# An early small write to the output: 128 rows in place of 16

**Chip, cores, metric.** One core of one Trainium2 chip. The metric is the device time of one execution in microseconds (us); lower is better.

## The reference

```python
def reference(x, y):                      # both (32, 256, 1024) float32
    batch, seq, dim = x.shape
    result = np.zeros((batch, seq, dim * 2), dtype=np.float32)
    result[..., 0::2] = x
    result[..., 1::2] = y
    return result
```

It interleaves two arrays. There is nothing to compute: 67.1 MB are read, 67.1 MB are written.

## The kernel before

The flat arrays are cut into 8 blocks of 128 rows of 8,192 elements. A block's x and y are loaded by SyncE's queue (SP), VectorE (DVE) copies them into every second place of an output tile, half a block at a time, and ScalarE's queue (ACT) stores that tile. x, y and output tiles have two buffers each. Ahead of the loop stands the small write that this study is about: zeros on top of the first store's rows, which the first store overwrites later.

```python
    wpool = ctx.enter_context(tc.tile_pool(name="wp", bufs=1))
    zero = wpool.tile([16, 128], fp32, name="zero")
    nc.vector.memset(zero, 0.0)
    first = dataclasses.replace(of, offset=0, ap=[[2 * WL, 16], [1, 128]])
    nc.scalar.dma_start(out=first, in_=zero)                  # L47

    start = 0
    for lw in lwidths:                                        # 8 blocks
        # ... tiles of this block, xs and ys: its rows in x and y
        nc.sync.dma_start(out=xtile, in_=xs)                  # L56
        nc.sync.dma_start(out=ytile, in_=ys)                  # L57
        soff = 0
        while soff < lw:                                      # 2 halves
            # ... otile, and os_: its 128 rows of 32,768 B in the output
            nc.vector.tensor_copy(out=otile[:, 0::2], in_=xsub)   # L70
            nc.vector.tensor_copy(out=otile[:, 1::2], in_=ysub)   # L71
            nc.scalar.dma_start(out=os_, in_=otile)               # L72
            soff += width
        start += P * lw
```

The program sets the semaphores by itself: the first store waits for the early write's landing, as both write the same rows.

## Time and profile before

| What | Before |
|---|---|
| time, 3 runs | 315.98 us median (315.83 to 316.15) |
| span of the profiled run | 313.8 us |
| VectorE busy | 72.8 us, 23% |
| DMA moved | 134.23 MB, 428 GB/s over the span |
| first store issued, its first packet | 24.32 us, 29.10 us |

The span is that of one profiled execution; the time has some 2 us more around it. VectorE, the only engine that computes, is idle for three quarters of the span, so the DMA engines, which move the data, are left to set this time. The prediction shows the lines behind it.

### The profile page before, as it was taken

What the parts mean: (1) busy time and instruction counts of PE and PEld (TensorE: products, weight loads), DVE (VectorE), ACT (ScalarE), POOL (GpSimd) and SP (SyncE); (2) the same over time, 40 slices, a digit from 0 to 9 for tenths busy, and PEclk for the clock granted to TensorE, in tenths of its full rate; (3) what the DMA queues carried; (4) which work ended last, traced back from release to release, by engine and by line L of the source; (5) the groups of instructions that cost most, each with busy time, mean ns of one, the idle gap of its engine ahead of it and who ended that gap; (6) DMA issues with size and microseconds to landing.
All of it is one profiled execution on the core that took longest, in us unless ns stands there. A gap on an engine that the chain in (4) does not pass through costs nothing.

```text
span 313.8 us, 152 instructions
## 1 busy us (share of the span) xinstructions
DVE 72.8 (23%) x33; POOL 0.2 (0%) x4
## 2 busy tenths in 40 slices
DVE  0433002231032410325003150130501305023500
POOL 0000000000000000000000000000000000000000
DMA  8999999999999999999999999999999999999997
GB/s 339 464 405 397 468 401 464 405 464 405 464 405 464 405 459 409 451 418 451 418 434 434 430 439 426 443 413 455 401 468 401 468 401 468 401 468 401 464 405 334
DMA packets 4640, 134.23 MB, mean 428 GB/s; under 512 B 528, under 2 KB 544, under 8 KB 544
## 3 DMA queue, kind: packets, MB, share of 16 engines
q1 hardware_dynamic: 2304, 67.11, 49.9%
q10 hardware_dynamic: 2336, 67.12, 49.5%
HBM read 67.11 MB, written 67.12 MB: 428 GB/s over the span
## 4 chain that ended last, share of the span: by engine, by line
DMA 83%; DVE 11%; DVEq 1%; issue 0%
DMA out_dram<-otile 76%; DMA ytile<-in_y_dram 7%; DVE otile L71 6%; DVE otile L70 5%; DVEq L83 1%; DVEq L70 0%
## 5 line engine op out<-in xcount | busy, mean ns | idle before, releaser
L70 DVE COPY otile<-xtile 128x4096 f32<-128x4096 f32 x16 | 36.6, 2295 | 184.9 <-DMA out_dram<-otile 173.7
L71 DVE COPY otile<-ytile 128x4096 f32<-128x4096 f32 x16 | 36.6, 2292 | 39.8 <-DMA ytile<-in_y_dram 39.8
L45 DVE MEMSET zero<- 16x128 f32 x1 | 0.2, 165 | 0.9 <-PEq L119 0.9
L119 POOL MEMSET const-bfloat16-1.0<- 128x1 bf16 x1 | 0.1, 102 | 0.0
L119 POOL MEMSET const-uint8-127<- 128x1 uint8 x1 | 0.1, 102 | 0.0
L119 POOL MEMSET const-float32-0.0<- 128x1 f32 x1 | 0.1, 99 | 0.2 <-issue 0.2
L119 POOL MEMSET const-float32-1.0<- 128x1 f32 x1 | 0.1, 99 | 0.0
## 6 DMA issues: line engine op xcount, KB each, us to landing
out_dram<-otile ACTq DMA_DIRECT2D x16, 4096.0 KB, 29.1
xtile<-in_x_dram SPq DMA_DIRECT2D x8, 4096.0 KB, 43.6
ytile<-in_y_dram SPq DMA_DIRECT2D x8, 4096.0 KB, 60.7
out_dram<-zero ACTq DMA_DIRECT2D x1, 8.0 KB, 6.3
```

Source lines behind the costliest of these rows:

```text
L45: nc.vector.memset(zero, 0.0)
L70: nc.vector.tensor_copy(out=otile[:, 0::2], in_=xsub)
L71: nc.vector.tensor_copy(out=otile[:, 1::2], in_=ysub)
L83: tc.compile()
L119: nc = _bacc.Bacc("TRN2", target_bir_lowering=False, num_devices=1)
```

## The change

The early write is to cover every row that the first store writes. The intent is presumably to warm something on the way to the output: with 16 rows the early write touched only 16 of the 128 rows that the first store writes, one packet for each of the 16 DMA engines; with 128 rows it touches them all, eight packets for each.

```diff
-    zero = wpool.tile([16, 128], fp32, name="zero")
+    zero = wpool.tile([P, 128], fp32, name="zero")
     nc.vector.memset(zero, 0.0)
-    first = dataclasses.replace(of, offset=0, ap=[[2 * WL, 16], [1, 128]])
+    first = dataclasses.replace(of, offset=0, ap=[[2 * WL, P], [1, 128]])
     nc.scalar.dma_start(out=first, in_=zero)
```

## The prediction

> **What bounds the kernel now.** I first read the page of the profile from the top, to see which engine is full.
>
> ```profile
> span 313.8 us, 152 instructions
> DVE 72.8 (23%) x33; POOL 0.2 (0%) x4
> ...
> DMA  8999999999999999999999999999999999999997
> ...
> DMA packets 4640, 134.23 MB, mean 428 GB/s; under 512 B 528, under 2 KB 544, under 8 KB 544
> ...
> q1 hardware_dynamic: 2304, 67.11, 49.9%
> q10 hardware_dynamic: 2336, 67.12, 49.5%
> ```
>
> VectorE, the only engine that computes, works 23% of the span. The 16 DMA engines are at 90% or more in 38 of the 40 slices, and the two queues (q1 has the loads, q10 the stores) together fill 99.4% of their time. So the kernel is bound by the bytes that it moves, and a wait somewhere else matters only if it leaves the DMA engines with nothing queued.
>
> The packet records of the trace say how tight that is. There are 4,096 packets of 32,768 B (one row of a tile each, 256 on each engine), and nearly all of them took 1.213 us: 32,768 B / 1.213 us = 27.0 GB/s on one engine, 432 GB/s on sixteen. 256 x 1.213 = 310.5 us is therefore the floor for this traffic at this rate. What the span has above that floor is 3.3 us. I looked for it by stretches of the span; the last two columns are the DMA share and the rate (a packet counts where it starts, so short stretches are uneven and the share can pass 1).
>
> ```profile
> 0.90:2.50 1.60, 0.13 (x1) 0.00 (x0) 1.00 1.20 328
> ...
> 11.30:25.80 14.50, 8.30 (x4) 0.00 (x0) 1.00 1.01 434
> 25.80:28.00 2.20, 0.69 (x1) 0.00 (x0) 1.00 1.39 477
> 28.00:30.00 2.00, 0.00 (x0) 0.00 (x0) 1.00 0.61 262
> ...
> 60.00:300.00 240.00, 59.02 (x26) 0.00 (x0) 1.00 1.00 433
> 300.00:313.80 13.80, 0.00 (x0) 0.00 (x0) 1.00 0.88 380
> ```
>
> From 60 to 300 us it runs at 433 GB/s with a share of 1.00: nothing to win. Two places are slow. One is the start: the first packet starts 0.99 us in, and the first round of load packets takes 1.47 to 2.27 us instead of 1.213. The other is the moment of the first big store: packets that start between 25.8 and 27.7 us take up to 1.88 us. By the packet records the time above 1.213 us is 0.71 us per engine in the first place (21 packets) and 0.64 us in the second (21 packets), and nowhere else is a big packet off 1.213 by more than 5 ns. The start (0.99), these two (1.35), the end (the last packet ends at 312.7 of 313.8, so 1.1) and the small packets account for the 3.3 us to within rounding.
>
> So the whole stretch that an early write to the output could possibly mend is the 0.64 us around the first store. Next, how the early write lies in the opening; the columns are start, length, engine, line and operation.
>
> ```profile
> 0.86 0.17 DVE L45 MEMSET zero<- 16x128 f32 x1 [0.86 <-PEq L119]
> 1.06 0.42 ACTq L47 DMA_DIRECT2D out_dram<-zero  x1
> ...
> 12.28 4.50 DVE L70 COPY otile<-xtile 128x4096 f32<-128x4096 f32 x2 [11.25 <-DMA xtile<-in_x_dram]
> 16.80 0.33 SPq L56 DMA_DIRECT2D xtile<-in_x_dram  x1
> 22.00 4.50 DVE L71 COPY otile<-ytile 128x4096 f32<-128x4096 f32 x2 [5.22 <-DMA ytile<-in_y_dram]
> 24.32 2.56 ACTq L72 DMA_DIRECT2D out_dram<-otile  x2
> ```
>
> ```profile
> out_dram<-zero ACTq DMA_DIRECT2D x1, 8.0 KB, 6.3
> ```
>
> The early write is issued at 1.06 us and lands 6.3 us later, near 7.4 us. ACT's queue holds the first store back until that landing (its semaphore wait ends at 7.42 us), because both write the same rows. But the first store cannot be issued before its second copy, which starts at 22.00 us when y has landed, is done at 24.3 us. The wait has 24.3 - 7.4 = 16.9 us of slack.
>
> **What the Trainium skill says.** All four places are on the page "DMA: Bandwidth & Descriptors".
> - "Where 436 GB/s comes from" gives 435.2 GB/s as the ceiling of 16 ports. The trace agrees: 432 GB/s in the packet records.
> - "Queues, rings and completion order": each engine goes round-robin between queue rows, a packet at a time. The trace agrees. Before 5.27 us an engine has only load packets; there each engine takes one 512 B packet of q10 in 27 ns, then one load packet of 1.213 us, then the 4 B semaphore packet at 6.50 us. During the first store, q10 and q1 alternate one 32 KB packet each.
> - "Why a DMA increments its semaphore by 16 and not by 1": the number of engines is the largest up to 16 that divides the slowest dimension on both sides. 16 rows give 16 engines with one row each, 128 rows give 16 engines with eight. The trace of before has 16 early packets and 16 increments; the 128-row case is seen in the big stores.
> - "Specifications" calls 512 B the smallest transfer at line rate, below which there is a read-modify-write. The new rows are still 512 B, so no new penalty should appear; before's took 27 ns each.
>
> **The change part by part.**
> 1. The memset goes from 16 to 128 partitions with 128 elements in each. Length per partition is the same, so I expect about 0.17 us again. Even ten times that would be nothing on the path, as VectorE idles until 12.28 us.
> 2. The DMA instruction on ACT: 0.42 us for 16 rows; the 128-row stores take 0.34 to 0.36 us. No gain or loss; ACT idles until 24.3.
> 3. The packets: 112 more of 512 B, 7 more on each engine, at 27 ns: 7 x 0.027 = 0.19 us of DMA time on every engine. It is the one term that lies on the path, because the engines are full before and after. It goes wholly to the time: +0.19 us.
> 4. The landing. If each row takes a turn between two load packets (0.027 + 1.213 = 1.24 us a turn), the seven further rows put the landing 7 x 1.24 = 8.7 us later: 15.0 us after issue, near 16.1 us. That is 8 us ahead of 24.3, so the first store's issue isn't delayed. Effect: 0.
> 5. The warming. The old write touched rows 0 to 15, one per engine, so not the rows that each engine then stores; the new one touches all 128 rows of the first store. If the 0.64 us of stretched packets come from a first touch of those rows, up to -0.64 us. I doubt it. All 16 engines are stretched alike, whether or not their rows were near the 16 already written; later stores also go to rows that nothing has touched, and their packets all take 1.213 us; and the early write itself cost the loads beside it nothing (1.211 to 1.226 us). I give it one chance in five, worth on average -0.1 us.
>
> Sum: 315.98 + 0.19 - 0.1 = 316.07, rounded to 316.1 us.
>
> **The rivals.**
> - *The cold write path is warmed row by row*: the first store's packets keep to 1.213 us, and the time is 315.98 + 0.19 - 0.64 = 315.5 us. For it: the stretch stands exactly where the first big store begins, as the other one stands at the first load. Against it: point 5.
> - *The cost is only moved*: the new rows do the first touch at 5 to 16 us, the load packets there stretch by the same 0.64 us, and the time stays at 316.2. For it: DMA is full then too, so a stall cannot hide.
> - *The early write becomes the wait that holds the first store.* If each small row must let two load packets pass, as the first one did, eight turns of 2.45 us end at about 5.3 + 19.6 = 24.9 us, and the store is issued 0.5 to 1 us late. Even so the DMA engines have the second pair of loads queued until 34 us, so nothing idles and the order merely shifts: 316.2 to 316.5. To cost 2% (6.3 us) the landing would have to slip past 34 us by as much again. Alternation one by one in the store phase speaks against even the mild form.
> - *The eight rows of an engine go as one packet*: landing stays near 6.3 us after issue, the same +0.19 us or somewhat less. The time can't tell this from my main line; the landing can.
>
> **Range and chances.** The known terms run from -0.45 (warming in full) to +0.5 (a delayed store). The three runs of before spread over 0.32 us by themselves, so 315.5 to 316.6 us should hold the result eight times in ten. A 2% gain would need 6.3 us, almost twice everything the span has above its floor of 310.5 us, so I give it 0.5%; a 2% loss needs DMA engines that idle for 6 us or small rows that cost thirty times their 27 ns: 1%.
>
> **What would show each step right or wrong.** In the changed kernel's profile: 4,752 packets (112 more) and 656 under 2 KB; q10 with 2,448; the early write at 64.0 KB with about 15.0 us to landing (6 to 8 would mean bursts, over 23 that it holds the store); the first issue of a store at 24.3 to 24.6 us; the stretched packets just before the first store's still summing to about 0.6 us per engine (gone if warming works, found at 5 to 16 us if moved); and a span of about 314.0. The prediction is wrong if the stretch is gone and the time is under 315.6, if the loads between 5 and 16 us slow by more than the 0.19 us, or if the rate of 433 GB/s in the middle of the span changes, for which I see no cause.

## The result

| | Before | After |
|---|---|---|
| time, 6 runs each | 316.12 us (315.83 to 316.93) | 316.24 us (315.71 to 317.0) |
| ratio after to before, 95% interval | | 0.9999 (0.9981 to 1.0017) |
| span of the profiled run | 313.8 us | 314.4 us |

A ratio here is the mean time of one kernel's fast runs over that of the other's of the same rounds, so it isn't quite the ratio of the medians above. The time is the same. The page of the changed kernel, in the lines that answer to those of before:

```profile
span 314.4 us, 152 instructions
...
DMA packets 4752, 134.29 MB, mean 427 GB/s; under 512 B 528, under 2 KB 656, under 8 KB 656
...
q1 hardware_dynamic: 2304, 67.11, 49.9%
q10 hardware_dynamic: 2448, 67.18, 49.5%
...
L45 DVE MEMSET zero<- 128x128 f32 x1 | 0.2, 165 | 0.9 <-PEq L119 0.9
...
out_dram<-zero ACTq DMA_DIRECT2D x1, 64.0 KB, 14.0
```

There are 112 packets more (4,752 against 4,640), all on q10 and all under 2 KB. The memset takes the same 165 ns for eight times the rows. The early write lands 14.0 us after its issue, not 6.3. Its packets took 27 ns each as before: the small packets' records sum to 0.51 us per engine, against 0.32, which is the 0.19 us of the prediction.

The opening by order of time (start, length, engine, line, operation):

```profile
1.07 0.40 ACTq L47 DMA_DIRECT2D out_dram<-zero  x1
...
12.61 4.50 DVE L70 COPY otile<-xtile 128x4096 f32<-128x4096 f32 x2 [11.57 <-DMA xtile<-in_x_dram]
...
22.31 4.50 DVE L71 COPY otile<-ytile 128x4096 f32<-128x4096 f32 x2 [5.20 <-DMA ytile<-in_y_dram]
24.64 2.56 ACTq L72 DMA_DIRECT2D out_dram<-otile  x2
```

The early write is down at 15.1 us and the first store is issued at 24.64 us, so it still waits for its own copy and not for the early write. It comes 0.3 us later than before because y does.

**How the stretch is read.** The last two load packets on each engine ahead of the first store took longer than 1.213 us. The stretch is this time above 1.213 us, summed over the packets and divided by the 16 engines. To see it in the page's form, take a window in which exactly these 32 packets start; the last figure of a queue's line is the time of its packets as a share of 16 engines' window. Before, from 25.8 to 28.0 us:

```profile
q1 hardware_dynamic: 32, 1.05, 139.2%
```

After, from 25.8 to 28.3 us:

```profile
q1 hardware_dynamic: 32, 1.05, 130.0%
```

Before: 1.392 x 2.2 us x 16 / 32 = 1.531 us a packet, two per engine, so 2 x (1.531 - 1.213) = 0.64 us of stretch. After: 1.300 x 2.5 x 16 / 32 = 1.625 us, so 0.82 us. The stretch has not gone; in this profile it is 0.2 us longer. It is the one figure that the change was to make smaller.

### The profile page after: what moved, and what is told of

It is laid out like the page before. It is cut to its first block, busy times and chain, and to the rows that moved or that the text cites. A ratio compares the mean times of both kernels' runs of the same rounds, so it can differ in the third digit from the quotient of the medians.

```text
span 314.4 us, 152 instructions
## 1 busy us (share of the span) xinstructions
DVE 72.8 (23%) x33; POOL 0.2 (0%) x4
## 2 busy tenths in 40 slices
DMA packets 4752, 134.29 MB, mean 427 GB/s; under 512 B 528, under 2 KB 656, under 8 KB 656
## 4 chain that ended last, share of the span: by engine, by line
DMA 83%; DVE 11%; DVEq 1%; issue 0%
DMA out_dram<-otile 76%; DMA ytile<-in_y_dram 7%; DVE otile L71 6%; DVE otile L70 5%; DVEq L83 1%; DVEq L70 0%
## 6 DMA issues: line engine op xcount, KB each, us to landing
out_dram<-otile ACTq DMA_DIRECT2D x16, 4096.0 KB, 29.1
xtile<-in_x_dram SPq DMA_DIRECT2D x8, 4096.0 KB, 43.6
```

## The experiments

Eleven further runs were made, nine of them of new kernels. The stretch is given by the packet records, per engine.

**1. The same kernels again.** No edit. The repeat of before is a single run, so its state is unknown (314.1 us of span and a time of 315.89 us put it beside the fast ones).

> The kernel before, unchanged, for the spread of the profile itself. In the first two profiles the load packets ahead of the first store were stretched by 0.64 us per engine (before) and 0.82 us (after). Theory A (the stretch is what a starting stream costs, and has nothing to do with the early write): here again 0.5 to 0.9 us, not necessarily 0.64. Theory B (the number of early rows changes it): 0.64 within 0.05. Time 315.7 to 316.9.

Measured: stretch 0.59 us. That lies within what both theories allow, so it only shows the spread.

> The changed kernel against the one before, with more rounds, for the size of the time difference and a second profile. Main theory: plus 0.19 us (112 more packets of 27 ns over 16 engines), ratio 1.0006, which five rounds may not part from 1; stretch 0.5 to 0.9 us and its difference to before not repeated. Rival (the stretch is really longer after the change): 0.82 us again, and the time up by 0.3 to 0.4 us (ratio 1.001).

Measured: ratio 0.9997 (0.9985 to 1.0009), stretch 0.96 us, span 314.4 us. A rise by more than 0.1%, as the rival had it, is outside the interval; the 0.06% of the main theory is inside, and so is nothing at all. The longer stretch did repeat, which the main theory did not expect.

**2. No early write at all.**

```diff
-    zero = wpool.tile([P, 128], fp32, name="zero")
-    nc.vector.memset(zero, 0.0)
-    first = dataclasses.replace(of, offset=0, ap=[[2 * WL, P], [1, 128]])
-    nc.scalar.dma_start(out=first, in_=zero)
```

> No early write at all. Theory A: the early write warms nothing, so the stretch before the first store is 0.5 to 0.9 us as with it, the start packets are as before, and the time is that of before less one packet of 27 ns: ratio 0.999 to 1.001. Theory B (the first touch of the output is dear and the 16 rows already took most of it away): the stretch or the delay from the first store's issue to its first packet (4.8 us in before) grows by 1 us or more and the time with it, ratio 1.003 or more.

Measured: ratio 1.0 (0.9987 to 1.0012), span 313.7 us, first store issued at 24.32 us and its first packet at 29.00 us, 4.7 us later as in before. The window from 25.8 to 28.0 us:

```profile
q1 hardware_dynamic: 32, 1.05, 137.1%
```

1.371 x 2.2 x 16 / 32 = 1.508 us a packet, 0.59 us of stretch. Theory B falls: the 16 rows of before did nothing either. The small write is idle weight in both kernels, and the simplest of the three has none.

**3. The 128 rows elsewhere.** The early write goes to the rows of the fifteenth of the sixteen stores.

```diff
-    first = dataclasses.replace(of, offset=0, ap=[[2 * WL, P], [1, 128]])
+    first = dataclasses.replace(of, offset=2 * (total - P * WL), ap=[[2 * WL, P], [1, 128]])
```

> The 128 early rows go into the place of the second last store's rows, so the first store finds none of its rows touched and is not held by their landing; the number of packets is that of the changed kernel. Theory A: stretch 0.5 to 0.9 us, time as the changed kernel's, ratio to before 1.000 to 1.001. Theory B (rows warm their own addresses): stretch before the first store as in the run without an early write and above that of before, and something shorter at the second last store, whose packets are all 1.213 us already.

Measured: ratio 0.9995 (0.9981 to 1.001), stretch 0.87 us, nothing at the fifteenth store. Whether the rows touched are the first store's own makes no difference: 0.82 and 0.96 us with them, 0.87 without.

**4. Eight small packets per engine, on 16 rows.** To tell the number of packets from the number of rows as the reason for the longer stretch.

```diff
+    SEGS = 8
-    zero = wpool.tile([P, 128], fp32, name="zero")
+    zero = wpool.tile([16, SEGS * 128], fp32, name="zero")
     nc.vector.memset(zero, 0.0)
-    first = dataclasses.replace(of, offset=0, ap=[[2 * WL, P], [1, 128]])
-    nc.scalar.dma_start(out=first, in_=zero)
+    first = dataclasses.replace(of, offset=0, ap=[[2 * WL, 16], [256, SEGS], [1, 128]])
+    nc.scalar.dma_start(out=first, in_=zero.rearrange("p (s e) -> p s e", s=SEGS))
```

> Eight early pieces of 512 B on each of 16 rows: as many small packets per engine as in the changed kernel (8), on as few rows as in before. The stretch before the first store was 0.59 to 0.64 us per engine with 0 or 1 early packets per engine, and 0.82 to 0.96 with 8. Theory (the number of small packets shifts the engines against each other): stretch 0.8 to 1.0 us, profiled span 314.2 to 314.5. Rival (the number of rows, so of addresses, does it): 0.55 to 0.65 us, span 313.7 to 314.2. Time within 0.15% of before in either case.

Measured: stretch 0.60 us, span 313.9 us, ratio 0.9991 (0.9974 to 1.0008). The window from 25.8 to 28.0 us:

```profile
q1 hardware_dynamic: 32, 1.05, 137.6%
```

The theory falls; the rival's figures hold. With no early write or 16 small rows the stretch was 0.59, 0.59, 0.60 and 0.64 us, with 128 small rows 0.82, 0.87 and 0.96. Why more rows should lengthen it isn't settled, and one run below (16 big rows, 0.80 us) fits neither group. The ratios can't tell the 0.25 us apart, as their intervals are wider.

**5. Four pieces on each of the 128 rows.** The landing is pushed past the point at which the first store is ready.

```diff
+    SEGS = 4
-    zero = wpool.tile([P, 128], fp32, name="zero")
+    zero = wpool.tile([P, SEGS * 128], fp32, name="zero")
     nc.vector.memset(zero, 0.0)
-    first = dataclasses.replace(of, offset=0, ap=[[2 * WL, P], [1, 128]])
-    nc.scalar.dma_start(out=first, in_=zero)
+    first = dataclasses.replace(of, offset=0, ap=[[2 * WL, P], [256, SEGS], [1, 128]])
+    nc.scalar.dma_start(out=first, in_=zero.rearrange("p (s e) -> p s e", s=SEGS))
```

> Early write of four separate 512 B pieces on each of the 128 rows: 32 small packets per engine in place of 8 (and 1). Main theory: 32 x 0.027 = 0.86 us against 0.03 in before, so plus 0.8 us (ratio 1.0026). One row per turn between load packets puts the landing at about 38 to 42 us, so the first store is held from about 25 to about 40 us, but loads for 58 us are queued, no engine idles and the hold costs nothing. Rival (the wait for the early write is paid in full once it passes 24.6 us): plus 13 to 17 us, ratio 1.045. Rival (small rows cost more than their 27 ns): more than plus 2 us.

Measured: ratio 1.0029 (1.0012 to 1.0046), 316.77 us. The first store was issued at 42.20 us, 17.6 us later than in the changed kernel, and no cost of that shows. The time of the hold (from, to, length, busy engines, clock, DMA share, GB/s):

```profile
24.60:42.20 17.60, 2.28 (x2) 0.00 (x0) 1.00 0.99 424
```

The DMA engines are full all through it: two pairs of loads and the third x are queued. The packets' records have 0.84 us more of small packets than before, and 0.27 us more stretch; the ratio says 0.9 us (0.4 to 1.5 by its interval). That fits 27 ns for a small row, and leaves next to nothing for holding the store while loads were queued. The stretch was still there, from 43.4 to 45.8 us:

```profile
q1 hardware_dynamic: 32, 1.05, 138.6%
```

1.386 x 2.4 x 16 / 32 = 1.663 us a packet, 0.90 us of stretch after 32 small packets per engine.

One thing was missed. SP's own queue waits, longest first (who, for what, total us, times, longest):

```profile
SPq L58 <- DMA out_dram<-zero: 24.8, 1, 24.8
```

The third y load (line 58 in this kernel) waits for the early write too. In the trace's records both have semaphore 101, and the queue waits on it before it issues that load. There is no common data, so the reason is presumably that the semaphore's earlier use has to be complete. Of the 24.8 us only the last 15.3 are due to it: y's buffer was in use by the copies until 26.88 us.

**6. Eight pieces on each row.** As run 5 with `SEGS = 8`.

> Eight 512 B pieces on each row: 64 small packets per engine, 1.73 us. Here the loads run out first: 6 tiles x 8 rows x 1.213 = 58 us of loads can be queued before a store lands. Main theory: the small packets take turns with loads until about 61 us, the rest go back to back, the write lands at 61 to 65 us and the first store is issued then; the DMA engines idle about 2 to 3 us between the landing and the first store's packet; total plus 1.7 + 2.5 = about plus 4 us (ratio 1.011 to 1.016). Rival (the hold is paid in full): first store 38 us late, ratio 1.12. Rival (hidden throughout): plus 1.7 us, ratio 1.005.

Measured: ratio 1.018 (1.0167 to 1.0193), 321.83 us, above the expected range. The landing came at 52.8 us and not at 61 to 65: as the third y load was held as well, only five tiles of loads were queued, 5 x 8 x 1.213 = 48.5 us and not 58. After that the small rows went back to back and the engines ran dry. Two windows around the landing:

```profile
50.00:52.90 2.90, 0.00 (x0) 0.00 (x0) 1.00 0.63 240
52.90:56.30 3.40, 0.00 (x0) 0.00 (x0) 1.00 0.73 154
```

By the packet records the last packet ends 6.1 us later than in before: 1.7 us of small packets, 2.0 us of idle engines, and 2.4 us of stretched packets, a part of them at 90 to 98 us, when the loads set in again after a pause. A pause alone doesn't do it: in run 5 the load queue paused too (76.4 to 88.0 us), and no packet was stretched there. The idle time was expected; the 2.4 us were not.

**7. The same eight pieces elsewhere.** Run 6, to the fifteenth store's rows.

```diff
-    first = dataclasses.replace(of, offset=0, ap=[[2 * WL, P], [256, SEGS], [1, 128]])
+    first = dataclasses.replace(of, offset=2 * (total - P * WL), ap=[[2 * WL, P], [256, SEGS], [1, 128]])
```

> The 64 small packets per engine of the eight-piece run, but written to the second last store's rows, so the first store does not wait for their landing (the second pair's y load still does, as it shares the early write's semaphore). Theory: of the plus 5.8 us of the eight-piece run only the packets' own 1.7 us are the bytes' price; the rest is the store held until the landing with nothing queued (2.0 us idle) and what restarting both streams together cost (some 2 us of stretched packets). With the store already queued: plus 1.7 to 3.3 us, ratio 1.005 to 1.0105, no idle stretch near 53 us. Rival (small packets cost more than 27 ns each, or the order in the ring is what costs): plus 5 us or more again.

(The held load is the third pair's y, not the second's as written there.) Measured: ratio 1.0037 (1.0011 to 1.0064), 317.19 us, a little under the expected range, with the interval reaching into it. The first store is issued at 24.56 us, stands in the queue behind the small rows, and starts at 51.7 us as soon as they are through. The two windows that were partly empty in run 6 are full:

```profile
50.00:52.90 2.90, 0.00 (x0) 0.00 (x0) 1.00 0.98 386
52.90:56.30 3.40, 0.00 (x0) 0.00 (x0) 1.00 1.07 463
```

The same packets in the same queue, without the first store's wait: plus 1.2 us in place of plus 5.7. So run 6 paid mostly for the wait with nothing queued and for the stretched packets after it, not for the small rows; and that the store's bytes start 22 us later than in before (51.7 against 29.1 us) costs next to nothing here. The stretch was 0.83 us in all, but in bits between 49 and 96 us. Ahead of the first store, which began as the last queued load packets ended, it was only 0.06 us, and at its issue there was none: the one first store after small rows that came without the usual stretch.

**8. 16 big rows.** One early packet per engine as in before, but of 15,872 B.

```diff
-    zero = wpool.tile([P, 128], fp32, name="zero")
+    zero = wpool.tile([16, 3968], fp32, name="zero")
     nc.vector.memset(zero, 0.0)
-    first = dataclasses.replace(of, offset=0, ap=[[2 * WL, P], [1, 128]])
+    first = dataclasses.replace(of, offset=0, ap=[[2 * WL, 16], [1, 3968]])
```

> Early write of 16 rows, one per engine as in before, but 15,872 B each in place of 512 B: at 27 GB/s 0.59 us more per engine. Theory A1 (the stretch is paid by each big store packet that starts while loads stream): load packets near the early write's start are stretched by 0.3 to 0.7 us per engine, and those before the first store by 0.5 to 0.9 us again; time plus 0.6 to 1.3 us. Theory B1 (the first big store pays once): stretch near the early write, and under 0.2 us before the first store; time plus 0.5 to 0.7 us. Theory C (the stretch belongs to the second copies or the DMA issues at 24 to 27 us, not to the store): nothing at the early write, 0.5 to 0.9 us at 26 us as ever.

Measured: ratio 1.0016 (1.0003 to 1.0029); stretch 0.09 us beside the early write and 0.80 us before the first store. The window from 26.3 to 28.7 us, 1.343 x 2.4 x 16 / 32 = 1.612 us a packet:

```profile
q1 hardware_dynamic: 32, 1.05, 134.3%
```

Too little at the early write for A1, too much later for B1; theory C, with nothing at the early write and 0.5 to 0.9 us later, comes near. C is half refuted by run 5, where the copies were long done and the stretch came with the store, at 43.6 to 47.4 us (0.90 us); but the third y load and both stores were issued together there too. Run 9 decides it: the same instructions are issued around its first store and there is no stretch.

**9. 128 big rows.** A store stream of its own, ahead of the first store: the tile of run 8 with `[P, 3968]`, written to `[[2 * WL, P], [1, 3968]]`.

> Early write of 128 rows of 15,872 B, 8 packets of 0.59 us per engine: a small store stream of its own, beside the loads, that ends before the first store. Its own packets cost 8 x 0.592 - 0.03 = plus 4.7 us (ratio 1.0149). Theory A1 (a stream of big packets that starts beside a running one costs 0.5 to 1 us): load packets are stretched by 0.3 to 1.0 us per engine near the early write's start (6 to 10 us) and by 0.5 to 1.0 again before the first store; plus 5.0 to 5.8 us. Theory B1 (paid once per kernel): stretch at the early write, under 0.2 us before the first store; plus 4.6 to 4.9 us. Neither: stretch under 0.15 us at the early write, as with 16 such rows, and 0.6 to 1.0 us at the first store.

Measured: ratio 1.0134 (1.0113 to 1.0154), 320.24 us. Two windows of 32 load packets, from 6.3 to 9.3 us beside the start of the early write, then from 30.9 to 33.3 us just before the first store:

```profile
q1 hardware_dynamic: 32, 1.05, 98.8%
```

```profile
q1 hardware_dynamic: 32, 1.05, 101.1%
```

The first is 0.988 x 3.0 x 16 / 32 = 1.482 us a packet, so 0.54 us of stretch (0.65 with the packets up to 12.2 us); the second 1.011 x 2.4 x 16 / 32 = 1.213 us, none at all. B1 holds: what the early stream paid, the first store did not pay again. The stretch over the whole opening (the start of the loads included) is 1.31 us per engine, against 1.34 in before, so it was moved and nothing was saved. The bytes of the big early write then cost what they take, 4.7 us by the packets, 4.2 by the ratio.

**10. 128 big rows elsewhere.** Run 9, to the fifteenth store's rows.

```diff
-    first = dataclasses.replace(of, offset=0, ap=[[2 * WL, P], [1, 3968]])
+    first = dataclasses.replace(of, offset=2 * (total - P * WL), ap=[[2 * WL, P], [1, 3968]])
```

> The early write of 128 rows of 15,872 B, moved to the second last store's rows. In the run before it, at the first store's own rows, some 0.6 us of stretch came at the early write (up to 12.2 us) and none before the first store. If the first big store stream pays once wherever it writes: again 1.2 to 1.4 us of stretch in the first 13 us (0.7 of it the start of the loads), under 0.1 us before the first store. If big writes had to warm the first store's own addresses: 0.5 to 1.0 us before the first store again. Time plus 4.0 to 5.5 us in both cases (ratio 1.0125 to 1.0175).

Measured: ratio 1.0134 (1.0109 to 1.016), 320.20 us. From 30.9 to 33.3 us, just before the first store:

```profile
q1 hardware_dynamic: 32, 1.05, 101.1%
```

None again, and 0.57 us at 5 to 13 us. So it is no matter of the addresses: in both runs the first stream of big store packets beside running loads stretched these by some 0.6 us, wherever it wrote. What is paid for is not settled. One packet of 15,872 B per engine was not enough to pay it (run 8), eight were, and 32 small ones were not (run 5, 0.90 us of stretch still at the first store). Run 6 can't be counted here: its 1.26 us came where loads and the first store both set in after idle time, and the start of the loads alone had 0.71 us in before. Nor is "once" a law: in run 6 another 1.6 us came when the loads set in again after a pause, and in run 7 the first store began with almost none. That stays open.

No version beat both kernels by more than the intervals.

## Why the prediction was right

The time was foretold as 316.1 us (315.5 to 316.6) and measured as 316.24. That the two lie 0.14 us apart is partly luck: six runs of one kernel spread over 1.1 to 1.3 us, and a sum of +0.19 and -0.1 us can't be seen in the ratio. What the runs do confirm is that nothing was won and nothing lost. By its steps:

- *The bound*: right, but its last sum isn't. 0.99 + 1.35 + 1.1 and the small packets' 0.32 make 3.8 us, not 3.3. The packet records of before overlap by 1.0 us per engine in all, so such parts add up only to about half a us. The 0.64 us of stretch, all that could be won, doesn't depend on it.

- *Memset and issue*: no cost. Right, 165 ns and 0.40 us.
- *Packets*: 112 more of 27 ns, 0.19 us per engine. Right in the packet records (0.51 against 0.32). In the time it can't be seen (the interval of run 1 is 0.24% wide), but four times as many rows gave 0.9 us against the 0.84 us of their packets (run 5).
- *Landing*: no delay of the first store. Right. Its size was off: 15.0 us after issue foretold, 14.0 measured. The failed term is "7 x 1.24". The eight rows did take turns one by one, but in one of these turns the load queue's packet was no 32 KB row. Two windows of the changed kernel show it, first from 10.2 to 11.1 us, a plain turn:

```profile
DMA packets 32, 0.53 MB, mean 592 GB/s; under 512 B 0, under 2 KB 16, under 8 KB 16
```

  and then from 11.4 to 12.3 us:

```profile
DMA packets 64, 0.54 MB, mean 601 GB/s; under 512 B 16, under 2 KB 48, under 8 KB 48
```

  The first has 16 small rows and 16 load packets. The second has two small rows on every engine (48 - 16 = 32), 16 load packets and 16 semaphore writes of 4 B: x's load was complete, its semaphore write of 9 ns took a turn of the load queue, and the next small row came at once. So there were six turns of 1.24 us and a short one, 7.5 us by the first semaphore packets (6.50 us before, 13.96 after).
- *Warming*: one chance in five, up to 0.64 us. It didn't come. The doubt was right (no early write at all gives the same stretch), and so was one reason given for it, that later stores to untouched rows show no stretch: runs 3 and 10 show that addresses don't matter. The sign for it, a stretch "still" of about 0.6 us, was met only roughly, with 0.82 and 0.96 us. (Its 1.211 to 1.226 us are of load packets before the early write, at 2.8 to 4.7 us; those beside it all took 1.213, which serves the reason as well.) That a big stream ahead of the first store pays the stretch in its place was not foreseen.
- *The waits*: incomplete. The prediction knew one waiter, the first store. The third y load waits for the same semaphore. In the changed kernel neither waited, as the first half of y was copied only at 24.6 us and the second at 26.8, both after the landing at 15.1 us; with 32 and 64 small rows per engine both did (runs 5 and 6).
- *The rivals*: the row-by-row warming is refuted (runs 2 and 3). "The cost is only moved" is wrong for small rows, where nothing moved, and right for big ones (run 9). "The early write becomes the wait" did not happen; run 5 shows that even the hold would have cost next to nothing, as argued. But loads were queued for longer than the 34 us named there: in run 6 the last of the five queued tiles ended near 51.9 us. "One packet" is refuted by the turns above.

## What to carry to other kernels

Where the DMA engines are full, first add up packet time against the span: here 310.5 of 313.8 us were packets at full rate, so no trick at the opening could win 2%. A warm-up write should be tested against none at all, as one that lands unnoticed may do nothing. The late landing here cost next to nothing while other transfers were queued (run 5), and some 4.5 us once they had run out (run 6 against run 7), so count the queued work, and look for every instruction that shares the semaphore, not only the one with the data hazard.

## What the Trainium skill lacked or had wrong

- "DMA: Bandwidth & Descriptors", "Queues, rings and completion order", calls 9 to 17 descriptors typical for the packet between two turns. Here a turn was one row: eight rows of 512 B took turns beside 32 KB load packets, six of them 1.24 us long. That a 4 B semaphore write takes a turn of its own (9 ns, and it let the next small row in 1.2 us early) is not said there.
- The same page, "Measured (HBM→SBUF, 128 partitions, SWDGE, issued from GpSimd)", has 64 KB in 0.95 us, for transfers into SBUF that GpSimd issues, and with the time before the first packet left out. The 64 KB write here, out of SBUF and beside a full load queue, took 14.0 us from issue to landing, 9.8 of them after its first packet at 5.30 us. So the table isn't refuted, but it has no row for a small transfer that takes turns with a full queue.
- The same page, "Latency and other measured facts", has about 600 ns to the first byte on this path. With nothing else running that fits: the first load packet came 0.99 us after its issue began, which itself took 0.37. Beside running loads, the first packet of the early write came 4.2 us after its issue (1.06 to 5.27 us) and that of the first store 4.8 us after.
- No page has the stretch ahead of the first stream of big store packets beside running loads: 0.59 to 0.96 us per engine, in loads stretched from 1.213 to 1.5 to 1.7 us a packet on average, gone from the first store when another such stream went ahead (runs 9 and 10). Its cause is open.
- The same page, "Why a DMA increments its semaphore by 16 and not by 1", warns of two DMAs in flight on one semaphore. What keeping them apart costs, it doesn't say: in run 5 SP's queue waited 24.8 us, 15.3 of them past the freeing of its buffer, for an early write with which its load has no data in common.
